# A second pair of blocks in seven products, and another order of gates, branches and output pairs

## The chip, the cores and the metric

The kernel runs on one core of one Trainium2 chip. The metric is the device time of one execution in microseconds (us), and the kernel before takes 769.0 us (median of three: 768.53, 769.0, 769.34). The core's engines are named as in the profile: PE is TensorE (matmuls and transposes), PEld its loads of weights, DVE is VectorE, ACT is ScalarE, POOL is GpSimd and SP is SyncE. POOL and SP do hardly more here than start transfers from device memory, each from a queue of its own.

## The reference

One layer over x of 256 tokens by 2048 channels, in float32:

```python
h = rms_norm(x, pre_norm_w)
proj = h @ w_in                       # 12304 columns, one combined projection
oa = gated_delta_rule(...)            # branch A, 8 heads of 128, from proj
ob = moba_attention(...) * silu(moba_z)   # branch B, 8 heads of 128, from proj
u_a = oa @ w_branch_a                 # 256 x 1024 by 1024 x 2048
u_b = ob @ w_branch_b                 # 256 x 1024 by 1024 x 2048
merged = sigmoid(gate_a) * u_a + sigmoid(gate_b) * u_b    # gates from proj, 2048 columns each
y = merged @ w_out                    # 256 x 2048 by 2048 x 2048
out = x + rms_norm(y, post_norm_w)
```

All that the change touches lies behind the two mixers, from `u_a` on.

## The kernel before, in words

**Precision.** TensorE multiplies at a reduced precision of float32, so each operand is split into a high part (a cast, on ScalarE) and a low part (the difference, on VectorE), and each product is three matmuls: high by high, high by low, low by high. `split` (line 221) does this for weights, 1024 elements a partition at a time, called a part below. It takes the tiles from a pool with three buffers, and every fourth part from a pool with one, so four parts can be in hand. Weights come in as 1 MB tiles `raw_...` from SP's queue, three buffers, two parts each.

**Blocks.** The 2048 columns of a gate, a branch or the output are four blocks of 512 columns; the 256 tokens are two halves. `proj_n` (line 347) computes one block the plain way: for each k tile of 128 and each token half, three matmuls of 512 columns into one PSUM bank. A gate block (k = 2048) is 96 matmuls, a branch block (k = 1024) 48.

**Seven products.** `seven` (line 815) computes two neighbouring blocks over 1024 rows of k at once. It treats token half by k half by column block as a 2 x 2 by 2 x 2 product and uses seven quarter products of 12 matmuls instead of eight, in four PSUM banks. For that it needs four sums of the left quarters (`s_`, each split into high and low) and sums of the weights' quarters (`tq`). The weights' sums are made by `prepare` (line 775): three fetches of 1 MB on GpSimd's queue, four additions on VectorE (`weight_sums`, line 763), and two transfers on GpSimd's queue that add a further quarter in place, one of them started inside `seven` behind product 6. In order of time `seven` runs products 1, 5, 6, 2, 7, 3, 4 and calls `fill(0)` after 1, `fill(1)` after 6, `fill(2)` after 7, `fill(3)` after 3: other products placed beside it, which give ScalarE and VectorE time, as each of its products has only 12 matmuls to two parts of weights. `product` (line 789) runs one such product, for one or two banks.

**Order.** The kernel's text fixes each engine's order. Small generators (`Queue`, line 47) issue side work: each is advanced by `tick`, twice a part, and says by its `yield` how many parts to wait (`T_WAIT` for the weights' sums). `ORDER` (line 43) lists the blocks of the combined projection and the calls of `branch_pair` (`ua0`, `ua1`). From the first branch on TensorE runs:

1. `ua0`: branch A, blocks 0 and 1, in seven products, beside it gate a block 3 (`gate_beside`, line 873);
2. gate b block 0 (`gb0`);
3. `ua1`: branch A, blocks 2 and 3, in seven, beside it gate b block 1;
4. branch B, blocks 0 and 1, the plain way (`branch`, line 1099); `weighted` (line 1089) multiplies them by the gate and adds the other branch; `merge` (line 1148) transposes the merged blocks, splits them, and makes the sums of their quarters;
5. gate b block 2;
6. output blocks 0 and 1, first half of k, in seven, beside it gate b block 3; the four banks are then copied away to SBUF ("parked", `park`, line 1195), as the second half of k needs branch B's last blocks;
7. output blocks 2 and 3, first half of k, in seven, beside it branch B blocks 2 and 3 (`branch_part`, line 1216);
8. the second half of k for output blocks 2, 0, 1 the plain way, the parked banks copied back ahead (`back`, line 1296), and block 3 with its weights split ahead (`last_parts`, `last`).

`weigh` (line 1243) squares a finished block on ScalarE and multiplies it by the norm's weight on VectorE; `finish` (line 1261) takes the root on ScalarE, scales and adds x on VectorE in five pieces, and sends each piece out, the pieces in turn on SP's and ScalarE's queue.

Of the kernel before, what the change touches and what calls it, by code (L numbers as in the profile page):

```python
# [27 lines left out]
T_WAIT = (5, 7, 7, 4)  # L28
# [15 lines left out]
    "q0 mv0 zg0 q1 kq2 kq3 zg1 v0 v1 v2 ga0 zm0 zm1 mv1 v3 mk0 mk1 mk2 mk3 ga1 ga2 ua0 gb0 ua1"  # L44
).split()

# [29 lines left out]
def hybrid_layer(  # L76
# [157 lines left out]
    hT = big.tile([P, KT, 2 * S], F32R, tag="hT", name="hT")  # L234
# [580 lines left out]
    def seven(quarter, s_, tq, w, c, banks, name, fill=lambda i: None, done=lambda b: None):  # L815
# [3 lines left out]
        fill(0)  # L819
        product([s_[0]], tq[0], [c12], [True], f"{name}p5")  # L820
# [32 lines left out]
    def branch_pair(i):  # L853
        c = 2 * i
        while not oas or not formed:
            sq.tick()
            gq.tick()
# [12 lines left out]
        gate = gate_beside(*(("ga", 3, CGA), ("gb", 1, CGB))[i])  # L870
        seven(quarters(oaT[0]), oas, tqs[-1], wa, c, (c11, c12, c21, c22), f"ua{c}", fill=gate, done=done)
# [15 lines left out]
    def next_sums(w, c):  # L887


        for q in aq + bq:  # L890
            q.drain()
        tq = [big.tile([P, 4, 512], F32, tag=f"z{i}", name=f"tq{len(tqs)}_{i}") for i in range(3)]
        prepare(tq, w, c, (2, 0, 1))

    def solve():
# [112 lines left out]
        tq = tg[:, 0], tz, tg[:, 1]  # L1008
# [100 lines left out]
    for blk in ORDER:  # L1109
# [17 lines left out]
        if n == "ua":  # L1127
            next_sums(*((wa, 2), (wo, 0))[c])
# [3 lines left out]

    mT = [big.tile([P, KT // 2, 2 * S], F32R, tag="u1", name="mT_0")]


    sums = [big.tile([P, 2, 4, P], F32R, tag=tg, name=f"sum_{tg}") for tg in ("tt", "tv", "tw")]
    SH = [tl[:, 0] for tl in sums] + [wk.tile([P, 4, P], F32R, tag="s", name="sum4_hi")]
    SL = [tl[:, 1] for tl in sums] + [wk.tile([P, 4, P], F32R, tag="s", name="sum4_lo")]
# [7 lines left out]
    summed, turned_blocks = [], []  # L1146

    def merge(c):
# [18 lines left out]
        if c == 1:  # L1167
# [9 lines left out]
            summed.append(True)  # L1177

    for c in range(2):
        branch(c)  # L1180
        mq.add(merge(c))
    sigmoid_gate("gb", CGB, 2)


    def ready(cond):
        while not cond():
            for q in (dq, sq, wq, mq):
                q.tick()

    ready(lambda: formed and summed)  # L1190
    first_half = quarters(mT[0])
# [24 lines left out]
    def branch_part(c, h):  # L1216
        if h == 0:

            if c == 3:
                ready(lambda: 2 in turned_blocks)  # L1220
            pbs[c] = [aux_tile(f"a_ub{c}_{t}") for t in range(NT)]
        product([ob(0, h), ob(1, h)], load(wb, h, c, "ub"), pbs[c], [h == 0] * 2, f"ub{c}_{h}")
        if h == 1:
            wq.add(weighted(c, pbs[c]))
            mq.add(merge(c))

    def beside_second(i):
        for c, h in (((2, 1),), ((3, 0),), ((3, 1),), ())[i]:
            branch_part(c, h)
# [142 lines left out]
```

## Time and profile before

| | |
|---|---|
| median of three executions | 769.0 us |
| the profiled execution | 769.19 us |
| its span | 767.5 us, TensorE granted 0.996 of full clock |
| TensorE busy | 758.3 us |
| VectorE, ScalarE busy | 564.9 us, 447.8 us |
| bytes moved | 162.36 MB, mean 212 GB/s |

The span is what the profile's records cover; the time is 1.7 us longer. A view by lines gives groups of instructions with their busy time, count and mean length; a view by windows gives the busy time of each engine in a stretch; the chain follows the instruction that ended last back through what released each step. Matmuls overlap, so their busy times add up to more than the time between their starts.

### The profile page before, as it was taken

The page shows a single profiled execution, that of the slowest core. Times are in us where ns is not written, and L with a number is a line of the kernel's source. Part 1 is how long each engine was busy: PE and PEld are TensorE (multiplying, and loading weights), DVE is VectorE, ACT ScalarE, POOL GpSimd, SP SyncE. Part 2 cuts the span into 40 slices and gives each one's busy share as a digit, 9 for nine tenths or more (in the row PEclk, how much of TensorE's full clock was granted, in tenths as well). Part 3 has the DMA queues.
Part 4 walks back from the last instruction along what each step waited for, and adds up shares of the span by engine and source line. Part 5 has one row for each costly group of instructions (what it writes and reads, how often), then busy time and mean ns, then how long its engine had stood idle before and what let it go on. Part 6 is the DMA issues. An engine that isn't in the chain of part 4 may idle for free.

```text
span 767.5 us, 10492 instructions
## 1 busy us (share of the span) xinstructions
PE 758.3 (99%) x3953; PEld 649.2 (85%) x3953; DVE 564.9 (74%) x920; ACT 447.8 (58%) x679; POOL 47.1 (6%) x73
## 2 busy tenths in 40 slices
PE   9999999999999999999999999999999999999995
PEld 8998988899888888888899888788888888888885
DVE  6877669885977898775457876676676976788664
ACT  6776666657655664554556474654555466665562
POOL 4000001112000000003001000100100000100000
PEclk9999999999999999999999999999999999999998
DMA  9585676458655557668437756886798497879732
GB/s 303 177 257 202 192 212 173 137 164 226 189 195 182 190 181 215 172 193 204 131 108 273 212 166 214 241 280 227 215 313 294 161 299 191 332 219 310 289 114 111
DMA packets 99321, 162.36 MB, mean 212 GB/s; under 512 B 3525, under 2 KB 49222, under 8 KB 98758
## 3 DMA queue, kind: packets, MB, share of 16 engines
q1 hardware_dynamic: 89766, 135.46, 54.3%
q0 software_dynamic: 8896, 25.18, 12.7%
q10 hardware_dynamic: 608, 1.06, 0.4%
q8 instruction: 31, 0.51, 0.3%
q14 instruction: 20, 0.16, 0.1%
HBM read 158.52 MB, written 3.15 MB: 211 GB/s over the span
## 4 chain that ended last, share of the span: by engine, by line
PE 96%; ACT 2%; DVE 1%; issue 0%; DVEq 0%; ACTq 0%
PE a_gb L148 11%; PE a_ga L148 11%; PE a_y L148 10%; PE a_zg L148 6%; PE a_mq L148 6%; PE a_v L148 6%; PE a_k L148 6%; PE a_mk L148 6%; PE a_ub L148 6%; PE a_zm L148 6%; PE a_mv L148 5%; PE a_ua L148 5%; PE a_q L148 4%; PE s L148 1%; PE ms L148 1%; PE po L148 1%
## 5 line engine op out<-in xcount | busy, mean ns | idle before, releaser
L148 PE MATMUL a_ga<-hi_ga,hT 128*128 128x512 f32 x256 | 82.1, 394 | 0.0
L148 PE MATMUL a_gb<-hi_gb,hT 128*128 128x512 f32 x256 | 81.5, 392 | 0.0
L148 PEld LDWEIGHTS a_gb<-hi_gb,hT 128*128 128x128 f32 x256 | 48.0, 188 | 10.5
L148 PEld LDWEIGHTS a_ga<-hi_ga,hT 128*128 128x128 f32 x256 | 48.1, 188 | 10.0
L227 DVE TENSOR_TENSOR lo_gb<-raw_gb,hi_gb 128x1024 fp32r<-128x1024 f32 x32 | 39.0, 1223 | 23.6 <-ACT hi_gb L226 23.2
L227 DVE TENSOR_TENSOR lo_ga<-raw_ga,hi_ga 128x1024 fp32r<-128x1024 f32 x32 | 39.0, 1223 | 19.8 <-ACT hi_ga L226 19.4
L226 ACT CAST hi_ga<-raw_ga 128x1024 fp32r<-128x1024 f32 x32 | 33.8, 1055 | 30.3 <-PE a_ga L148 17.4
L148 PE MATMUL a_ga<-lo_ga,hT 128*128 128x512 f32 x128 | 50.1, 391 | 0.1
L226 ACT CAST hi_gb<-raw_gb 128x1024 fp32r<-128x1024 f32 x32 | 33.5, 1051 | 28.3 <-PE a_gb L148 18.0
L148 PE MATMUL a_gb<-lo_gb,hT 128*128 128x512 f32 x128 | 50.0, 391 | 0.0
L148 PE MATMUL a_zg<-hi_zg,hT 128*128 128x348 f32 (+1 forms) x192 | 47.1, 322 | 0.0
L148 PE MATMUL a_mq<-hT,hi_mq 128*128 128x512 f32 x128 | 47.0, 407 | 0.0
L148 PE MATMUL a_mk<-hT,hi_mk 128*128 128x512 f32 x128 | 46.2, 402 | 0.0
L148 PE MATMUL a_q<-hT,hi_q 128*128 128x512 f32 x128 | 45.9, 398 | 0.0
L148 PE MATMUL a_v<-hT,hi_v 128*128 128x512 f32 x128 | 45.3, 398 | 0.0
L148 PE MATMUL a_ub<-hi_ub,obT 128*128 128x512 f32 x128 | 40.8, 392 | 0.0
L148 PE MATMUL a_k<-hT,hi_k 128*128 128x512 f32 x128 | 40.8, 401 | 0.0
L148 PE MATMUL a_zm<-hi_zm,hT 128*128 128x512 f32 x128 | 40.5, 392 | 0.0
L148 PE MATMUL a_mv<-hi_mv,hT 128*128 128x512 f32 x128 | 40.1, 391 | 0.0
L148 PE MATMUL a_v<-hT,lo_v 128*128 128x256 f32 x128 | 36.0, 282 | 0.0
L148 PE MATMUL a_q<-hT,lo_q 128*128 128x256 f32 x128 | 35.9, 280 | 0.0
L148 PE MATMUL a_mq<-hT,lo_mq 128*128 128x256 f32 x128 | 35.9, 280 | 0.0
(398 smaller groups left out, 2008.6 us busy)
## 6 DMA issues: line engine op xcount, KB each, us to landing
raw_ga<-in_w_in_dram SPq DMA_DIRECT2D x16, 1024.0 KB, 5.2
raw_gb<-in_w_in_dram SPq DMA_DIRECT2D x16, 1024.0 KB, 5.2
raw_y<-in_w_out_dram SPq DMA_DIRECT2D x14, 1024.0 KB, 8.6
raw_q<-in_w_in_dram SPq DMA_DIRECT2D x8, 1024.0 KB, 5.6
raw_mv<-in_w_in_dram SPq DMA_DIRECT2D x8, 1024.0 KB, 5.1
raw_v<-in_w_in_dram SPq DMA_DIRECT2D x8, 1024.0 KB, 5.7
raw_zm<-in_w_in_dram SPq DMA_DIRECT2D x8, 1024.0 KB, 5.1
raw_mq<-in_w_in_dram SPq DMA_DIRECT2D x8, 1024.0 KB, 5.7
```

The lines of the kernel that those rows point to most:

```text
L148: return pin(nc.tensor.matmul(*args, **kwargs))
L226: nc.scalar.copy(hi, raw)
L227: nc.vector.tensor_tensor(lo, raw, hi.bitcast(F32), op=ALU.subtract)
```

## The change

Branch B's blocks 0 and 1 are computed by `seven` too. Its left sums are new: `input_sums` joins the attention output's high and low parts, makes the four sums on VectorE and splits them again. Its weights are prepared in the second half of the gate b tile, which is still empty, and two other tiles. The order on TensorE becomes: `ua0` with gate a block 3; `ua1` with gate b block 0; gate b block 1; branch B blocks 0 and 1 in seven with gate b block 2; branch B block 2; gate b block 3; output blocks 0 and 1, first half of k, in seven, with branch B block 3 beside products 1 and 6 and nothing beside the last ones; output block 0, second half; output blocks 2 and 3, first half, in seven, with the rest of output blocks 0 and 1 beside it; output block 2, second half; block 3. No bank is parked. The wait for sums moves into `seven`, ahead of product 5. A square root of a constant is taken behind the last gate. All pieces of the first token half go out by SP's queue. The tile of the normed input becomes two tiles of half its size, each reused on its own.

```diff
-T_WAIT = (5, 7, 7, 4)
+T_WAIT = (5, 4, 4, 7)
...
 ORDER = (
-    "q0 mv0 zg0 q1 kq2 kq3 zg1 v0 v1 v2 ga0 zm0 zm1 mv1 v3 mk0 mk1 mk2 mk3 ga1 ga2 ua0 gb0 ua1"
+    "q0 mv0 zg0 q1 kq2 kq3 zg1 v0 v1 v2 ga0 zm0 zm1 mv1 v3 mk0 mk1 mk2 mk3 ga1 ga2 ua0 ua1"
...
-    hT = big.tile([P, KT, 2 * S], F32R, tag="hT", name="hT")
+    hT = Halves(*(big.tile([P, KT // 2, 2 * S], F32R, tag=f"hT{i}", name=f"hT_{i}") for i in range(2)))
...
         s5 = tq[0][:, 0]
         product([quarter(0, 0)], load(w, 0, c, name), [c21], [True], f"{name}p1")
         fill(0)
+        while not (formed and s_):
+            for q in (dq, sq, iq, wq, mq):
+                q.tick()
         product([s_[0]], tq[0], [c12], [True], f"{name}p5")
         nc.scalar.copy(c11, c21)
         product([s_[1]], tq[1], [c21], [False], f"{name}p6")
...
     def branch_pair(i):
         c = 2 * i
-        while not oas or not formed:
+        while not oas:
             sq.tick()
...
-        gate = gate_beside(*(("ga", 3, CGA), ("gb", 1, CGB))[i])
-        seven(quarters(oaT[0]), oas, tqs[-1], wa, c, (c11, c12, c21, c22), f"ua{c}", fill=gate, done=done)
+        gate = gate_beside(*(("ga", 3, CGA), ("gb", 0, CGB))[i])
+        def beside(j):
+            if j == 3:
+                if i == 0:
+                    z = [z_tile(k, "ua2") for k in range(3)]
+                    prepare(z, wa, 2, (0, 1, 2))
+                else:
+                    gb23 = gb_tile()[:, 2:4].rearrange("p c t n -> p (c t) n")
+                    prepare((gb23, z_tile(0, "ub"), z_tile(2, "ub")), wb, 0, (0, 2, 1))
+            gate(j)
+        seven(quarters(oaT[0]), oas, tqs[-1], wa, c, (c11, c12, c21, c22), f"ua{c}", fill=beside, done=done)
+        if i == 1:
+            iq.add(input_sums())
...
-    def next_sums(w, c):
-        for q in aq + bq:
-            q.drain()
-        tq = [big.tile([P, 4, 512], F32, tag=f"z{i}", name=f"tq{len(tqs)}_{i}") for i in range(3)]
-        prepare(tq, w, c, (2, 0, 1))
+    def z_tile(i, name):
...
+    iq = Queue()
+    extra.append(iq)
+    ob_sums = []
...
+    def input_sums():
+        hi, lo = sum_tiles("obs")
+        l = big.tile([P, 4, 4, P], F32, tag="z1", name="obs_f")
+        l = [l[:, i] for i in range(4)]
+        quarter = quarters(obs[0])
...
+        def part(i):
+            nc.scalar.copy(hi[i], l[i])
+            nc.vector.tensor_tensor(lo[i], l[i], hi[i].bitcast(F32), op=ALU.subtract)
+        yield 2
+        whole(2, 1, 0)
+        whole(0, 1, 1)
+        yield 1
+        less(0, 2, 0)
+        whole(1, 0, 0)
+        yield 1
+        less(2, 1, 2)
+        whole(3, 0, 1)
+        yield 1
+        less(1, 0, 1)
+        part(0)
+        yield 1
+        nc.vector.tensor_tensor(l[3], l[3], l[1], op=ALU.add)
+        part(1)
+        yield 1
+        part(2)
+        yield 1
+        part(3)
+        ob_sums.extend(zip(hi, lo))
...
-        tq = tg[:, 0], tz, tg[:, 1]
+        tq = tg[:, 0], tg[:, 1], tz
...
-        if n == "ua":
-            next_sums(*((wa, 2), (wo, 0))[c])
...
+    sigmoid_gate("gb", CGB, 1)
+    bb = [acc_tile(f"a_ub0_{n}") for n in ("11", "12", "21", "22")]
+    ready_halves = []
+    def weighted_half(b):
+        i = next(i for i in range(4) if bb[i] is b)
+        c, t = i % 2, i // 2
+        nc.vector.tensor_tensor(gb_tile()[:, c, t, :], gb_tile()[:, c, t, :], b, op=ALU.mult)
+        nc.vector.tensor_tensor(ga(c, t), ga(c, t), gb_tile()[:, c, t, :], op=ALU.add)
+        ready_halves.append(c)
+        if ready_halves.count(c) == 2:
+            merged.append(c)
+    ob = quarters(ob_tile())
+    seven(ob, ob_sums, tqs[-1], wb, 0, bb, "ub", fill=gate_beside("gb", 2, CGB), done=weighted_half)
+    prepare([z_tile(i, "y") for i in range(3)], wo, 0, (1, 2, 0))
...
     for c in range(2):
-        branch(c)
         mq.add(merge(c))
-    sigmoid_gate("gb", CGB, 2)
...
-    gate = gate_beside("gb", 3, CGB)
+    branch(2)
+    sigmoid_gate("gb", CGB, 3)
+    root = wk.tile([P, 1], F32, tag="rstd", name="root")
+    pin(nc.scalar.activation(root, epst, AF.Sqrt))
+    while not merged[1:]:
+        wq.tick()
+    mT.append(big.tile([P, KT // 2, 2 * S], F32R, tag="hT0", name="mT_1"))
+    mq.add(merge(2))
+    first_half, second_half = quarters(mT[0]), quarters(mT[1])
     banks = [acc_tile(f"a_y0_{n}") for n in ("11", "12", "21", "22")]
-    def park(b):
-        nc.scalar.copy(freed(next(i for i in range(4) if banks[i] is b)), b)
+    pb = [aux_tile(f"a_ub3_{t}") for t in range(NT)]
     def beside_first(i):
-        if i == 3:
+        if i < 2:
+            product([ob(0, i), ob(1, i)], load(wb, i, 3, "ub"), pb, [i == 0] * 2, f"ub3_{i}")
+        if i == 1:
+            wq.add(weighted(3, pb))
+            mq.add(merge(3))
+            spare = big.tile([P, 2, 4, 512], F32, tag="hT1", name="tq_y2")
             ga01 = ga_[:, 0:2].rearrange("p c t n -> p (c t) n")
-            tq = [big.tile([P, 4, 512], F32, tag=f"z{j}", name=f"tq_{j}") for j in (0, 2)]
-            prepare((tq[0], ga01, tq[1]), wo, 2, (1, 0, 2))
-        gate(i)
-    seven(first_half, list(zip(SH, SL)), tqs[-1], wo, 0, banks, "y", fill=beside_first, done=park)
-    parked = [freed(i) for i in range(4)]
-    tail = big.tile([P, KT, 2 * S], F32R, tag="hT", name="mT_1")
-    mT.append(tail[:, : KT // 2])
-    ob = quarters(ob_tile())
-    pbs = {}
-    def branch_part(c, h):
-        if h == 0:
-            if c == 3:
-                ready(lambda: 2 in turned_blocks)
-            pbs[c] = [aux_tile(f"a_ub{c}_{t}") for t in range(NT)]
-        product([ob(0, h), ob(1, h)], load(wb, h, c, "ub"), pbs[c], [h == 0] * 2, f"ub{c}_{h}")
-        if h == 1:
-            wq.add(weighted(c, pbs[c]))
-            mq.add(merge(c))
-    def beside_second(i):
-        for c, h in (((2, 1),), ((3, 0),), ((3, 1),), ())[i]:
-            branch_part(c, h)
-    c21, c11, c12, c22 = (acc_tile(f"a_y2_{n}") for n in ("21", "11", "12", "22"))
-    branch_part(2, 0)
-    ready(lambda: formed)
-    seven(first_half, list(zip(SH, SL)), tqs[-1], wo, 2, (c11, c12, c21, c22), "y", fill=beside_second)
+            tq_next.extend((spare[:, 0], ga01, spare[:, 1]))
+            fetch(tq_next, wo, 2, (0, 2, 1))
+    tq_next = []
+    seven(first_half, y_sums, tqs[-1], wo, 0, banks, "y", fill=beside_first)
...
-            (nc.sync if i % 2 == 0 else nc.scalar).dma_start(of[t * P : (t + 1) * P, cs], yw[t][:, cs])
...
+            (nc.sync if t == 0 or i % 2 == 0 else nc.scalar).dma_start(of[t * P : (t + 1) * P, cs], yw[t][:, cs])
+    def rest(c, h, pts):
+        product([second_half(t, h) for t in range(NT)], load(wo, 2 + h, c, "y"), pts, [False, False], f"y{c}_{h}")
...
-    second_half = quarters(mT[1])
-    def rest(c, h, banks):
-        product([second_half(t, h) for t in range(NT)], load(wo, 2 + h, c, "y"), banks, [False, False], f"y{c}_{h}")
-    def back(c, bank):
-        pts = [bank(f"a_y{c}_{t}") for t in range(NT)]
-        for t in range(NT):
-            nc.scalar.copy(pts[t], parked[2 * t + c])
-        return pts
-    ready(lambda: 2 in turned_blocks)
-    rest(2, 0, (c11, c21))
     ready(lambda: 3 in turned_blocks)
-    y0 = back(0, aux_tile)
-    rest(0, 0, y0)
-    last_parts(2)
-    rest(2, 1, (c11, c21))
-    rest(0, 1, y0)
+    formed.clear()
+    sq.add(weight_sums(tq_next, wo, 2, 0))
+    c11, c22 = pb
+    c21, c12 = (aux_tile(f"a_y2_{n}") for n in ("21", "12"))
+    def beside_second(i):
+        if i == 0:
+            rest(0, 1, (banks[0], banks[2]))
+        elif i < 3:
+            rest(1, i - 1, (banks[1], banks[3]))
+        else:
+            last_parts(2)
+        if i == 1:
+            for t in range(NT):
+                weigh(0, t, banks[2 * t])
+    rest(0, 0, (banks[0], banks[2]))
+    seven(first_half, y_sums, tq_next, wo, 2, (c11, c12, c21, c22), "y", fill=beside_second)
+    hx = big.tile([P, NT, D], F32, tag="u1", name="hx")
+    for t in range(NT):
+        weigh(1, t, banks[1 + 2 * t])
+    for h in range(2):
+        rest(2, h, (c11, c21))
+        if h == 0:
+            last_parts(3)
+            nc.sync.dma_start(hx, xf.rearrange("(t p) d -> p t d", p=P))
     for t in range(NT):
         weigh(2, t, (c11, c21)[t])
-    y1 = back(1, acc_tile)
-    rest(1, 0, y1)
-    for t in range(NT):
-        weigh(0, t, y0[t])
-    rest(1, 1, y1)
-    last_parts(3)
-    nc.sync.dma_start(hx, xf.rearrange("(t p) d -> p t d", p=P))
-    for t in range(NT):
-        weigh(1, t, y1[t])
```

More of the change, by code (lines that the diff above doesn't have):

```diff
@@ L43, with __init__, __getitem__ @@
 ORDER = (
-    "q0 mv0 zg0 q1 kq2 kq3 zg1 v0 v1 v2 ga0 zm0 zm1 mv1 v3 mk0 mk1 mk2 mk3 ga1 ga2 ua0 gb0 ua1"
+    "q0 mv0 zg0 q1 kq2 kq3 zg1 v0 v1 v2 ga0 zm0 zm1 mv1 v3 mk0 mk1 mk2 mk3 ga1 ga2 ua0 ua1"
 ).split()
+class Halves:
+    def __init__(self, *halves):
+        self.halves = halves
+    def __getitem__(self, i):
+        p, k, *rest = i
+        n = self.halves[0].shape[1]
+        first = k.start if isinstance(k, slice) else k
+        o = first // n * n
+        k = slice(k.start - o, k.stop - o) if isinstance(k, slice) else k - o
+        return self.halves[first // n][(p, k, *rest)]
 class Queue:
@@ L1176, in merge @@
                 nc.vector.tensor_tensor(SL[i], sf[j], SH[i].bitcast(F32), op=ALU.subtract)
-            summed.append(True)
+            y_sums.extend(zip(SH, SL))
     for c in range(2):
-        branch(c)
         mq.add(merge(c))
-    sigmoid_gate("gb", CGB, 2)
[L1185 to L1191, printed above, removed]
-    gate = gate_beside("gb", 3, CGB)
+    branch(2)
@@ L1239, in hybrid_layer @@
     yw = [big.tile([P, D], F32, tag=f"z{1 - t}", name=f"yw_{t}") for t in range(NT)]
-    hx = big.tile([P, NT, D], F32, tag="u1", name="hx")
     ssy = [cst.tile([P, 4], F32, name=f"ssy_{t}") for t in range(NT)]
@@ L1283, in last_parts @@
         raw = load(wo, kb, 3, "y")
+        tl = big.tile([P, 2, 2, 2, 512], F32R, tag=("g0", "hT1")[kb - 2], name=f"keep_{kb}")
         for u in range(2):
-            hi, lo = keep[len(parts)]
+            hi, lo = tl[:, u, 0], tl[:, u, 1]
             pin(nc.scalar.copy(hi, raw[:, 2 * u : 2 * u + 2, :]))
```

24 lines of the change are left out of this document (16 added, 8 removed).

## The prediction

> **What bounds the kernel now.** First the page: busy time, and the chain that ended last. Then that chain in order of time, and stretches of the span, to see whether TensorE ever waits where the change works.
>
> ```profile
> span 767.5 us, 10492 instructions
> PE 758.3 (99%) x3953; PEld 649.2 (85%) x3953; DVE 564.9 (74%) x920; ACT 447.8 (58%) x679; POOL 47.1 (6%) x73
> PE 96%; ACT 2%; DVE 1%; issue 0%; DVEq 0%; ACTq 0%
> ```
>
> ```profile
> core 0: us, PE busy (x) PEld busy (x) DVE busy (x) ACT busy (x) POOL busy (x), PEclk, DMA share, GB/s
> 480.00:506.00 26.00, 25.92 (x115) 20.94 (x114) 17.69 (x18) 17.00 (x21) 2.06 (x2) 1.00 0.84 260
> 506.00:585.00 79.00, 79.00 (x347) 64.74 (x346) 54.25 (x51) 43.83 (x46) 5.62 (x6) 1.00 0.83 265
> 585.00:631.00 46.00, 46.00 (x210) 37.80 (x210) 37.53 (x43) 22.80 (x28) 2.10 (x2) 1.00 0.73 226
> 631.00:687.00 56.00, 56.00 (x246) 45.77 (x245) 40.93 (x38) 35.35 (x40) 4.13 (x4) 1.00 0.84 267
> 687.00:715.00 28.00, 28.00 (x131) 23.01 (x130) 24.17 (x26) 18.21 (x21) 1.86 (x2) 1.00 0.72 226
> 715.00:755.00 40.00, 40.00 (x184) 33.10 (x183) 21.65 (x27) 20.64 (x34) 0.00 (x0) 1.00 0.50 184
> ```
>
> From 480 us to 755 us TensorE is busy all but 0.08 us, at full clock. So a matmul taken out is worth its whole slot, and a new wait costs its whole length. VectorE is next: 24.17 of 28 us in the busiest stretch.
>
> **The matmuls.** The chain prices a slot, and shows one quarter product (12 matmuls), one whole gate block (96) and the transposes of one half block:
>
> ```profile
> 522.32 21.96 PE a_gb L148 x96
> 544.28 2.76 PE a_ua L148 x12
> 585.46 20.56 PE a_ub L148 x90
> 606.02 0.44 PE mt L151 x4
> ```
>
> 20.56 / 90 = 0.229 us a matmul of 512 columns. Blocks 0 and 1 of the second branch are 96 matmuls now; seven quarter products of 12 are 84. The order listing of both programs has 3820 and 3808 TensorE matmuls and transposes: the 12 are the whole difference, since the other pairs were in seven products already. **12 x 0.229 = 2.75 us go.** A matmul lasts 0.39 us in the page's groups, but they overlap; the slot counts.
>
> **The new VectorE work.** The input sums are 12 instructions of 512 elements a partition on VectorE, with four casts on ScalarE; four weights' sums and the product's two corrections come on top. The weights split for each product are VectorE's main load. What an instruction costs in a row of them:
>
> ```profile
> 607.72 1.27 DVE L1092 TENSOR_TENSOR gb<-gb,a_ub 128x512 f32<-128x512 f32 x2
> 712.09 3.49 DVE L227 TENSOR_TENSOR lo_y<-raw_y,hi_y 128x1024 fp32r<-128x1024 f32 x3
> 627.02 1.22 DVE L227 TENSOR_TENSOR lo_yp<-raw_y,hi_yp 128x1024 fp32r<-128x1024 f32 x1
> 628.16 0.68 DVE L1176 TENSOR_TENSOR sum_lo<-gb,sum_hi 128x512 fp32r<-128x512 f32 x1
> 608.32 1.05 ACT L226 CAST hi_gb<-raw_gb 128x1024 fp32r<-128x1024 f32 x1
> 609.26 0.59 ACT L1161 CAST mT<-mt 128x512 fp32r<-128x512 f32 x1
> ```
>
> Two of 512 take 1.27 us, three of 1024 take 3.49 us: in a row they overlap by about 0.08 us, so a 512 costs 0.605 us and a 1024 1.14 us, the last of a row its full 0.68 or 1.22. A cast costs ScalarE 0.94 us (608.32 to 609.26). A part of weights (two k tiles) can be cast only once TensorE is through with the part four before it. With these I laid VectorE's new order against TensorE's, place by place:
>
> 1. *Second pair of the first branch* now follows the first pair with no gate block between. When TensorE ends the first pair's last product, VectorE has the last weighting (0.605), a weights' sum (1.14) and the gate's first low part (1.22): 2.97 us, some 0.2 us after that end, since the result must first be seen. TensorE wants it after 2.75 + 0.23 = 2.98 us. **Wait 0.2 us.**
> 2. *Gate block 1* (22 us): eight low parts, four weights' sums, the weighting and the 12 input-sum instructions: 12 x 1.14 + 13 x 0.605 = 21.5 us in 22.0 us, and VectorE enters up to four parts (5 us) ahead. No wait. The sums end some 12 us before product 5 needs them.
> 3. *Gate block 3.* Let S be the start of branch block 2 on TensorE. Its four transposes (0.44 each) stand inside. The cast of gate part 3 waits for branch part 3: S + 3 x 2.75 + 3 x 0.44 = S + 9.6, with a copy ahead S + 9.9; its low part ends the VectorE queue's claim at S + 12.1. Then stand 12 instructions of 512 (merge, sums of merged quarters, weighting of block 2), one weights' sum, and the low part of gate part 4: 12 x 0.605 + 1.14 + 1.22 = 9.62, so S + 21.7. TensorE wants it at S + 11.0 + 1.76 + 3 x 2.75 + 0.23 = S + 21.2. **Wait 0.5 us**; the next part has 0.605 + 1.14 + 1.22 = 2.97 us against 2.75: **0.2 us** more.
> 4. *End of the first output pair.* Nothing is placed beside its products 3 and 4 any more, so small products, whose 1.14 us low part serves 1.375 us of TensorE, follow each other. Let U be the end of the last branch block's third part. VectorE is free for the run at U + 2.25; 7 x 0.605 + 12 x 1.14 + 1.22 = 19.1 bring it to the second pair's first low parts at U + 21.4. TensorE wants those at U + 2 x 2.75 + 3 x 2.75 + 2 x 0.44 + 5.5 + 1.375 + 0.23 = U + 21.7. No wait, 0.3 us to spare.
>
> Together **+0.9 us**. That such lateness costs TensorE its length is seen once in the trace of before:
>
> ```profile
> 483.24 0.39 PE L148 MATMUL a_ga<-hi_ga,hT 128*128 128x512 f32 x1
> 483.71 0.50 PE L148 MATMUL a_ga<-lo_ga,hT 128*128 128x512 f32 x1
> ```
>
> 0.47 us from start to start instead of 0.23. It stands ahead of the change's first difference, and stays. Bounds of the 0.9: 0 if VectorE is earlier than I laid it; with no overlap at all (0.08 on each instruction) places 1, 3 and 4 give 0.4 + 1.5 + 0.4 + 1.2 = 3.5 us. The overlap is measured, so I stay at 0.9.
>
> **Parking** (four copies out, four back, ScalarE, 0.6 us each) goes: no wait of TensorE stands there in the rows above, so 0 us (bounds 0 and, for one copy back ahead of a product, 0.6 gained). The split of the input's tile into halves, the wait counts and the loop that now holds product 5 back in the writing of the program issue nothing: they set the order and free the half tiles, 0 us.
>
> **The root ahead, and the output queue.** The table load moves from the end to behind the last gate:
>
> ```profile
> 754.68 1.28 ACT L1263 ACT_TABLE_LOAD   x1
> 755.98 0.29 ACT L1263 ACTIVATE rs<-ssy,rb_True 128x1 f32<-128x1 f32 x1
> 756.50 2.87 DVE L1268 SCALAR_TENSOR_TENSOR yw<-yw,rs,hx 128x256 f32<-128x256 f32 x5
> 757.68 1.66 ACTq L1272 DMA_DIRECT2D out_dram<-yw  x2
> 756.59 1.60 PE L148 MATMUL a_y22b<-mT 128*128 128x256 f32 x12
> 758.03 1.60 PE L148 MATMUL a_y22b<-keep,mT 128*128 128x256 f32 x12
> 759.39 0.38 ACT L1248 ACTIVATE jy<-a_y 128x256 bf16<-128x256 f32 x1 [3.12 <-DVE yw L1268]
> 760.48 0.29 ACT L1263 ACTIVATE rs<-ssy,rb_False 128x1 f32<-128x1 f32 x1 [0.25 <-DVE rb_False L1258]
> ```
>
> The 1.28 us is no 1.28 us of gain: the first half of the rows finishes beside TensorE's last products, which end at 758.03 + 1.60 = 759.63, and the second half follows those. What does reach the end: ScalarE, held by two output transfers of the first half, squares a quarter, that was ready when the next began at 756.59, only at 759.39, and the last root waits 0.25 us for what hangs on it. All first-half transfers are SP's now, so ScalarE squares early: **-0.3 us** (bounds 0 and 0.4). At its new place the load delays the cast of the last branch block's second part; two sigmoids (0.6 each), load, root (0.3), two casts (0.5 each), this part's cast and low part are 1.2 + 1.28 + 0.3 + 1.0 + 1.05 + 1.22 = 6.05 us. TensorE wants it 2.75 + 0.88 + 2.75 + 0.23 = 6.6 us after the gate's end, and the first sigmoid starts three matmuls before that end: about 1 us to spare, 0 us.
>
> [...]
>
> **Transfers.** GpSimd's queue gets a fifth set of weights to sum (three fetches and two adding transfers each, 1 MB apiece); SP has one load of weights fewer.
>
> ```profile
> raw_y<-in_w_out_dram SPq DMA_DIRECT2D x14, 1024.0 KB, 8.6
> tq<-in_w_out_dram POOLq DMA_DIRECT2D x8, 1024.0 KB, 8.2
> ga<-in_w_out_dram POOLq DMA_DIRECT2D x2, 1024.0 KB, 9.9
> 560.00:580.00 20.00, 20.00 (x89) 1.00 1.03 359
> ```
>
> On GpSimd's queue the fetch into the second half of the gate tile waits for the first pair's last low part and holds the adding transfer of the second pair behind it, which is wanted some 20 us later: 8.2 us are hidden. Tightest is product 4 of the first output pair: its adding transfer starts after product 6's last low part, and 12.8 us later its cast is due; 8.2 to 9.9 us fit. 0 us.
>
> **Sum:** -2.75 + 0.9 - 0.3 = -2.15. The profiled execution took 769.19 us beside its 767.5 us span, so 767.0; it stands 0.19 over the median of 769.0. Against the median: **766.9 us**.
>
> **The rivals.**
> - *No new wait* (VectorE keeps its lead): 769.0 - 2.75 - 0.3 = 765.9. For it: before has none in 275 us but 0.24. Against: place 3. Chance 0.10.
> - *VectorE eats the gain.* Its instructions take 0.05 us more each in places 3 and 4 (dependent ones wait for each other, say): 16 x 0.05 and 19 x 0.05 - 0.3, about 1.5 us more: 768.4. Without overlap 769.5. For it: place 4 is 19 us of unbroken VectorE work. Chance 0.20.
> [...]
> - *Slower: the output weights come late.* From product 2 of the first output pair to the load of the block beside the second pair's product 1, TensorE runs 26 us, and five loads, three adding transfers and the norm weights' broadcast must land: 9 x 1.05 = 9.44 MB, 363 GB/s. At the 359 GB/s moved in 560 to 580 us this just fits; the load I find tightest has 12 us against the 8.6 us of the row, 3.4 to spare. At 270 GB/s it takes 35 us: 9 - 3.4 = 5.6 us of waiting, 772.5. It ends over 770.5 once 3.6 + 3.4 = 7 us are lost, from 9.44 MB / 33 us = 286 GB/s down. For it: the stage's mean of 267 GB/s; against: that is what was asked for there, not a limit. Chance 0.09.
> - *The change doesn't take the 12 out of the path*: excluded by the order listing and the full TensorE.
>
> **The numbers.** Forecast 766.9, its own range 766.3 to 767.5, chance 0.58. 0.2% is 1.5 us, about what a measurement here can tell from no change, so faster means under 767.5: 0.10 + 0.03 + 0.50 of the forecast = 0.63; slower (over 770.5) 0.09; the rest, 0.28, is the same. From the no-wait case to most of the case in which VectorE eats the gain: 765.8 to 769.3.
>
> **What would show it.** Right: 84 matmuls of the second branch's first pair; TensorE full but for three gaps, 0.2 us at the second pair's first gate part, 0.5 and 0.2 us in gate block 3; no table load in the last 15 us; the end 7.5 us behind the last matmul instead of 7.8. Wrong: ScalarE idle ended by transfers of output weights that TensorE then waits for, or gaps in the first output pair's last products.

## The result, and the profile after

The changed kernel takes **766.8 us** (median of 9 runs, 766.49 to 767.21), the kernel before 768.84 us (9 runs beside it, 768.36 to 769.34). The ratio is 0.9973, with a 95% interval of 0.9964 to 0.9982: 2.0 us, or 0.27%, are gone. Forecast were 766.9 us.

The busy times on the page of the changed kernel, whose span is 765.1 us:

```profile
PE 755.9 (99%) x3941; PEld 646.3 (84%) x3941; DVE 583.2 (76%) x944; ACT 452.7 (59%) x684; POOL 52.0 (7%) x78
```

TensorE has 12 instructions fewer (3953 before), VectorE 24 more and 18.3 us more work. The same view of the span in stretches as for the kernel before:

```profile
core 0: us, PE busy (x) PEld busy (x) DVE busy (x) ACT busy (x) POOL busy (x), PEclk, DMA share, GB/s
506.00:585.00 79.00, 78.88 (x345) 64.31 (x344) 67.26 (x69) 44.87 (x49) 6.99 (x7) 1.00 0.88 277
631.00:687.00 56.00, 55.64 (x254) 45.23 (x253) 45.40 (x51) 34.07 (x42) 5.46 (x6) 1.00 0.83 264
687.00:715.00 28.00, 28.00 (x128) 23.04 (x127) 24.78 (x25) 19.03 (x24) 2.60 (x2) 1.00 0.83 239
655.00:681.00 26.00, 26.00 (x119) 21.41 (x119) 18.14 (x18) 16.87 (x21) 2.84 (x3) 1.00 0.98 302
```

Two stretches have idle time of TensorE, 0.12 and 0.36 us (585 to 631 us has none). The timeline of TensorE shows where (each row: start, length, engine, line, what is written from what; in brackets how long the engine was idle and for whom):

```profile
483.31 0.50 PE L163 MATMUL a_ga<-lo_ga,hT 128*128 128x512 f32 x1
524.48 0.39 PE L163 MATMUL a_gb<-hi_gb,hT 128*128 128x512 f32 x1
524.98 0.50 PE L163 MATMUL a_gb<-lo_gb,hT 128*128 128x512 f32 x1
647.40 0.61 PE L163 MATMUL a_gb<-hi_gb,hT 128*128 128x512 f32 x2
648.38 0.50 PE L163 MATMUL a_gb<-lo_gb,hT 128*128 128x512 f32 x1 [0.36 <-DVE lo_gb L242]
648.72 0.63 PE L163 MATMUL a_gb<-hi_gb,hT 128*128 128x512 f32 x2
754.61 3.04 PE L163 MATMUL a_y22b<-keep,mT 128*128 128x256 f32 x24
```

At 524 us a matmul starts 0.50 us behind the one before instead of 0.23: a gap of 0.27 us. At 647 us two slots last 0.98 instead of 0.46: 0.52 us. The first is at the first low part of the gate block beside the second pair, the forecast's place 1; the second is at the fourth part's low part in gate block 3, its place 3. The slot behind each gap is longer too: 524.98 to 525.32 and 648.38 to 648.72, 0.34 us instead of 0.23.

The best measure of a change here is the time from the last matmul that both kernels wait for in the same place (the first low part at 483 us, ahead of the change) to the end of the last matmul. I call it the work. Before it was 483.71 to 759.63, 275.92 us; now it is 483.31 to 754.61 + 3.04 = 757.65, 274.34 us: **1.58 us less**. Behind it, 1.07 us instead of 1.38 pass from the end of the last matmul to the beginning of the last five output operations: 0.31 less. This is the tail below; the expectations count it up to the end of the span, 7.45 and 7.8 us. The five operations now, then in the kernel before:

```profile
758.72 2.87 DVE L1336 SCALAR_TENSOR_TENSOR yw<-yw,rs,hx 128x256 f32<-128x256 f32 x5
```

```profile
761.01 2.87 DVE L1268 SCALAR_TENSOR_TENSOR yw<-yw,rs,hx 128x256 f32<-128x256 f32 x5
```

Together 1.9 of the 2.0 us. The profiled pair also differ by 0.40 us *ahead* of 483 us, where the change only gives tiles other places.

### The profile page after: what moved, and what is told of

Its sections match the earlier page's. It is cut to its first block, busy times and chain, and to the rows that moved or that the text cites. A ratio compares the mean times of both kernels' runs of the same rounds, so it can differ in the third digit from the quotient of the medians.

```text
span 765.1 us, 10514 instructions
## 1 busy us (share of the span) xinstructions
PE 755.9 (99%) x3941; PEld 646.3 (84%) x3941; DVE 583.2 (76%) x944; ACT 452.7 (59%) x684; POOL 52.0 (7%) x78
## 4 chain that ended last, share of the span: by engine, by line
PE 94%; DVE 3%; ACT 2%; issue 0%; DVEq 0%
PE a_ga L163 11%; PE a_gb L163 10%; PE a_y L163 9%; PE a_ub L163 6%; PE a_zg L163 6%; PE a_mq L163 6%; PE a_v L163 6%; PE a_mk L163 6%; PE a_k L163 6%; PE a_zm L163 6%; PE a_mv L163 6%; PE a_q L163 4%; PE a_ua L163 4%; PE s L163 1%; PE ms L163 1%; PE po L163 1%
## 5 line engine op out<-in xcount | busy, mean ns | idle before, releaser
L163 PE MATMUL a_mk<-hT,lo_mk 128*128 128x256 f32 x128 | 35.8, 280 | 0.0
```

Source lines behind the costliest of these rows:

```text
L163: return pin(nc.tensor.matmul(*args, **kwargs))
```

## The experiments

All are edits of the changed kernel. "Work" is as above; the changed kernel has 274.34 us of it.

**1. The seven products undone in the second branch.**

```
-    seven(ob, ob_sums, tqs[-1], wb, 0, bb, "ub", fill=gate_beside("gb", 2, CGB), done=weighted_half)
+    branch(0)
+    sigmoid_gate("gb", CGB, 2)
+    branch(1)
...            (and no prepare(..., wb, ...), no input_sums(); T_WAIT (5, 4, 7, 7), for one set of sums fewer)
```

> The changed kernel with one part undone: blocks 0 and 1 of the second branch are computed as two plain blocks of 48 matmuls again, in their new place in the order; their weights' sums, the input sums and the adding transfer are gone. TensorE has 12 matmuls more than the changed kernel. Theory (the 12 matmuls are taken out of a path that TensorE sets): 12 x 0.229 = 2.75 us more, less the part of the 0.52 us wait in gate block 3 that goes because VectorE has fewer instructions ahead of it, so 2.3 to 2.75 us over the changed kernel's 766.8, 769.1 to 769.6, with the end of the work still 7.45 us behind the last matmul. Rival (VectorE's work for the seven products eats most of the gain, in waits too short to stand in a row of their own): at most 1.3 us more, 768.1 or less.

Measured: 769.96 us, ratio to the kernel before 1.0013 (1.0004 to 1.0022), 3.2 us over the changed kernel. The work is 483.08 to 757.56 + 3.04 = 760.60, 277.52 us, 3.18 more. That is a little over the theory's span, and far from the rival. TensorE's timeline shows why it is over 2.75 us: the plain form has waits too, at the fourth low part of gate block 3 and, new, at a low part of the last branch block.

```profile
483.08 0.50 PE L163 MATMUL a_ga<-lo_ga,hT 128*128 128x512 f32 x1
650.49 0.50 PE L163 MATMUL a_gb<-lo_gb,hT 128*128 128x512 f32 x1 [0.18 <-DVE lo_gb L242]
671.40 0.50 PE L163 MATMUL a_ub<-lo_ub,obT 128*128 128x512 f32 x1 [0.25 <-DVE lo_ub L242]
757.56 3.04 PE L163 MATMUL a_y22b<-keep,mT 128*128 128x256 f32 x24
```

Counted with the longer slots behind them, and with place 1's gap, which stays, its waits come to 1.5 us, those of the changed kernel to 1.1. So 2.8 us of the 3.18 are the 12 matmuls, against 2.75 by their slots. The run also says that the rest of the change, without the 12, makes the kernel 1 us slower than the one before (769.96 against 768.91 us beside it).

**2 and 3. The weights' sums in gate block 3, earlier and later.**

```
-T_WAIT = (5, 4, 4, 7)
+T_WAIT = (5, 4, 4, 5)        # 2: two half products earlier
+T_WAIT = (5, 4, 4, 8)        # 3: one half product later
```

> The changed kernel with one number changed: the sums of the first output pair's weights, four VectorE instructions of 1024 elements a partition, begin two half products earlier (wait count 5 instead of 7), while the merged quarters are still being summed in gate block 3. The instructions and their number stay. Theory (the 0.52 us gap is TensorE waiting for the fourth low part, because VectorE has a full queue ahead of it, and every 1024 ahead of it costs its 1.14 us): two such instructions now stand ahead of the low part instead of being one and then spread, so the gap grows by 2 x 1.14 = 2.28 to 2.8 us, and the time to 766.8 + 2.2 = 769.0. Rival (TensorE's short gaps are made up for later, or the weights' sums are not what stands ahead of the low part): gap and time as in the changed kernel, 766.8.

> The changed kernel with the same number moved the other way: the sums of the first output pair's weights begin one half product later (wait count 8 instead of 7). Theory: the weights' sum of 1.14 us no longer stands ahead of the late low part, and both gaps in gate block 3 go (0.52 and about 0.1 us in the changed kernel's trace), the 0.27 us gap at the second branch pair's first gate part stays: 766.8 - 0.6 = 766.2. The sums now end one half product later and the adding transfer of the output weights starts that much later; with 8 us from issue to landing and the first output pair's products more than 10 us behind, nothing else waits. Rival (the low part is late for another reason, the four merged sums' casts for one): the gap stays, 766.8. Rival that ends slower: the adding transfer lands late and product 7 of the first output pair waits, a gap of up to 1.4 us behind 668 us.

Measured: earlier 770.58 us (769.23 to 771.82, ratio 1.0019, 1.0010 to 1.0028), later 767.13 us (ratio 0.9975, 0.9965 to 0.9985).

With the sums earlier the gap is as long as forecast. TensorE's timeline, and the granted clock in the 2 us behind the wait (the column after POOL's):

```profile
482.90 0.50 PE L163 MATMUL a_ga<-lo_ga,hT 128*128 128x512 f32 x1
646.95 0.61 PE L163 MATMUL a_gb<-hi_gb,hT 128*128 128x512 f32 x2
650.19 0.79 PE L163 MATMUL a_gb<-lo_gb,hT 128*128 128x512 f32 x1 [2.62 <-DVE lo_gb L242]
650.78 1.05 PE L163 MATMUL a_gb<-hi_gb,hT 128*128 128x512 f32 x2
651.64 0.63 PE L163 MATMUL a_gb<-lo_gb,hT 128*128 128x512 f32 x1
757.57 3.04 PE L163 MATMUL a_y22b<-keep,mT 128*128 128x256 f32 x24
```

```profile
650.00:652.00 2.00, 1.81 (x4) 1.49 (x5) 2.00 (x4) 0.00 (x0) 0.00 (x0) 0.50 1.14 210
```

From 646.95 to 650.19 stand two slots and 2.78 us of waiting, 2.26 more than in the changed kernel: two sums of 1.14 us, to within 0.02. But the work, 482.90 to 760.61, grew by 3.37 us (the median by 3.8). The rest is the clock: behind this wait TensorE is granted 0.50, and the next slots last 0.43 us (650.78 to 651.64 are two). In this execution a wait of 2.8 us costs 1.1 us more than its length. It is no fixed price: the ten executions take 769.23 us at a granted clock of 0.997 over the whole span up to 771.82 us at 0.993. Here a wait of 2.8 us, 2.62 us of it shown as idle, was enough for the half clock. The waits of about 1 us in the runs below left the clock at 1.00 (1.02 us in run 3, granted 1.00 in 669 to 672 us; 1.06 us in run 7, granted 1.00 in 695 to 698 us); what a wait between 1.06 and 2.8 us does, these runs do not show.

With the sums later both gaps in gate block 3 are gone, as the theory said, and yet the time is not shorter: a new gap of 1.02 us stands at the second low part of the last branch block. TensorE, then ScalarE ahead of it:

```profile
668.94 0.50 PE L163 MATMUL a_ub<-lo_ub,obT 128*128 128x512 f32 x1 [0.77 <-DVE lo_ub L242]
662.00 1.05 ACT L241 CAST hi_ub<-raw_ub 128x1024 fp32r<-128x1024 f32 x1 [4.91 <-DMA raw_ub<-in_w_branch_b_dram]
662.95 1.26 ACT L759 ACTIVATE gb<-a_gb,rstd 128x512 f32<-128x512 f32 x2
664.22 1.28 ACT L1280 ACT_TABLE_LOAD   x1
665.51 0.20 ACT L1280 ACTIVATE root<-epst 128x1 f32<-128x1 f32 x1
665.62 1.05 ACT L1256 CAST mT<-mt 128x512 fp32r<-128x512 f32 x2
666.56 1.07 ACT L241 CAST hi_ub<-raw_ub 128x1024 fp32r<-128x1024 f32 x1
```

ScalarE has been idle 4.91 us when the block's first weights land. Then comes an unbroken row: the cast, the two sigmoids, **the table load of the root ahead**, the root, two casts, and only then the second cast for that block. This is the row that the forecast priced for the root's new place, with one thing missing: that a transfer sets its beginning.

In the changed kernel the same row starts with the same kind of wait, and TensorE just gets through:

```profile
661.44 1.05 ACT L241 CAST hi_ub<-raw_ub 128x1024 fp32r<-128x1024 f32 x1 [3.51 <-DMA raw_ub<-in_w_branch_b_dram]
662.40 1.25 ACT L759 ACTIVATE gb<-a_gb,rstd 128x512 f32<-128x512 f32 x2
667.11 1.23 DVE L242 TENSOR_TENSOR lo_ub<-raw_ub,hi_ub 128x1024 fp32r<-128x1024 f32 x1 [0.15 <-ACT hi_ub L241]
668.76 0.39 PE L163 MATMUL a_ub<-lo_ub,obT 128*128 128x512 f32 x1
```

The low part ends at 667.11 + 1.23 = 668.34 and is used at 668.76: 0.4 us to spare. The 0.52 us wait ahead of it had been covering this one. Not all of run 3's 1.02 us was uncovered, though: in its profile the row also starts 0.56 us later (662.00 against 661.44), and why the weights landed later there was not tried. Run 4, below, has the same wait count in this place; its row starts at 661.27 us, and a gap comes all the same.

**4 and 5. All three new gaps, and then the table load.** In 4 the sums of the first branch's second pair are also taken out of the way of place 1; in 5 the root ahead goes as well.

```
-T_WAIT = (5, 4, 4, 7)
+T_WAIT = (5, 2, 4, 8)        # 4 and 5
...
-    root = wk.tile([P, 1], F32, tag="rstd", name="root")
-    pin(nc.scalar.activation(root, epst, AF.Sqrt))        # 5 only
```

> The changed kernel with two wait counts changed: the output weights' sums one half product later as in the run before (8 instead of 7), and the sums of the first branch's second pair two half products earlier (2 instead of 4), so that none of them stands between the last weighting of the first pair and the first low part of the gate block beside the second pair. Theory: all three gaps that the change brought go (0.27, 0.52 and about 0.1 us), 766.8 - 0.9 = 765.9, which is the forecast's rival without any new wait. Rival: VectorE is as full in the neighbouring products, so the waits only move to other low parts, and the time stays at 766.8.

> The run with both wait counts moved (5, 2, 4, 8), with one part of the change undone beside it: no root of a constant is taken ahead, so the table load stands before the first half's root at the end again. In that run a new gap of 0.78 us had come at the last branch block: its second low part follows a ScalarE chain that begins with the first cast of that block's weights, which a late transfer sets (661.27 us), and has the 1.28 us table load and the 0.2 us root in it. Theory (the load in this chain is what makes the low part late): ScalarE is 1.28 + 0.11 = 1.4 us earlier with the second cast, the gap of 0.78 us goes, and since the first half's root has 3 us before the last matmul, the load costs nothing at the end: tail 7.45 us as before, time 766.65 - 0.8 = 765.9. Rival (the weights' transfer itself is too late, and the first low part of the block waits for it): a gap stays at the block's first or second low part, 766.4 to 766.7. Rival on the end (the load holds back the second half's squares): tail about 7.8 us, 766.3.

Measured: 4 takes 766.65 us (ratio 0.9971, 0.9960 to 0.9983), 5 takes **765.82 us** (765.74 to 766.07, ratio 0.9961, 0.9948 to 0.9973). In 4 the gaps at 524 and 647 us are gone and one of 0.78 us from start to start stands behind the table load. So its theory was wrong; the rival had the time, and that the wait moves, but not the cause, which is ScalarE's row and not a full VectorE. In 5 no new gap is left. The gap in 4, then the rows of 5: TensorE, the two casts of the block's weights, and the last five operations (the table load now stands at 751.72 us):

```profile
668.21 0.50 PE L163 MATMUL a_ub<-lo_ub,obT 128*128 128x512 f32 x1 [0.62 <-DVE lo_ub L242]
```

```profile
483.46 0.50 PE L163 MATMUL a_ga<-lo_ga,hT 128*128 128x512 f32 x1
753.63 3.04 PE L163 MATMUL a_y22b<-keep,mT 128*128 128x256 f32 x24
661.69 1.05 ACT L241 CAST hi_ub<-raw_ub 128x1024 fp32r<-128x1024 f32 x1 [4.73 <-DMA raw_ub<-in_w_branch_b_dram]
663.79 1.04 ACT L241 CAST hi_ub<-raw_ub 128x1024 fp32r<-128x1024 f32 x1
757.74 2.87 DVE L1334 SCALAR_TENSOR_TENSOR yw<-yw,rs,hx 128x256 f32<-128x256 f32 x5
```

The weights still end a long idle time of ScalarE, 4.73 us, but the second cast now starts 2.1 us behind the first instead of 4.6 (in run 3's rows). The work is 483.46 to 756.67, 273.21 us. This gives the price of two terms at once. Against the kernel before (275.92) it is 2.71 us less: the 12 matmuls, 2.75 by their slots. Against the changed kernel it is 1.13 us less: what its waits cost. And the tail is 757.74 - 756.67 = 1.07 us, as in the changed kernel: with the load back at the end nothing is lost. Run 5 beats both kernels, by 1.0 us the changed one: its five times all lie below the nine of the changed kernel, which were not taken beside them, and the work says the same.

**6 and 11. The end.** In 6 the first half's output pieces go out on both queues again, with the root still ahead; 11 is run 5 with that same edit, so that both parts that touch the end are undone.

```
-            (nc.sync if t == 0 or i % 2 == 0 else nc.scalar).dma_start(of[...], yw[t][:, cs])
+            (nc.sync if i % 2 == 0 else nc.scalar).dma_start(of[...], yw[t][:, cs])
```

> The changed kernel with one part undone: the first half's output pieces go out on SP's and ScalarE's queues in turn again, as before the change; the root stays ahead. Theory (ScalarE, held by the two transfers of the first half, squares a quarter late, and the last root waits for it): the tail behind the last matmul grows from 7.45 to 7.8 us, 766.8 + 0.35 = 767.15. Rival (what shortened the tail is that the table load no longer delays the first half, so that VectorE and ScalarE are through with it before the last matmul ends): tail 7.45 us, 766.8, since the first half's pieces are now ready 2.5 us earlier than in the kernel before.

> The fastest run so far (5, 2, 4, 8, root at the end, 765.8 us) with the first half's output pieces on both queues again: now both parts of the change that touch the end are undone. Each alone left the tail at 7.45 us. Theory (either part suffices: with the load at the end, the first half is finished 1.28 us later, and only then are ScalarE's two transfers still to be issued when the second half's quarter is ready for its square): tail 7.8 us, as in the kernel before, 766.2. Rival (the 0.37 us of the tail come from neither part): tail 7.45 us, 765.8.

Measured: 6 takes 766.79 us (ratio 0.9975, 0.9964 to 0.9986), nothing lost, as its rival had it; 11 takes 766.17 us (ratio 0.9962, 0.9949 to 0.9976), 0.35 us more than 5, as its theory had it. The square of the second half's first quarter and the last five operations, in 6 and then in 11:

```profile
754.64 3.04 PE L163 MATMUL a_y22b<-keep,mT 128*128 128x256 f32 x24
756.44 0.38 ACT L1316 ACTIVATE jy<-a_ub 128x256 bf16<-128x256 f32 x1 [3.39 <-DVE yw L1336]
758.75 2.87 DVE L1336 SCALAR_TENSOR_TENSOR yw<-yw,rs,hx 128x256 f32<-128x256 f32 x5
```

```profile
753.73 3.04 PE L163 MATMUL a_y22b<-keep,mT 128*128 128x256 f32 x24
756.53 0.38 ACT L1314 ACTIVATE jy<-a_ub 128x256 bf16<-128x256 f32 x1 [3.12 <-DVE yw L1334]
758.15 2.87 DVE L1334 SCALAR_TENSOR_TENSOR yw<-yw,rs,hx 128x256 f32<-128x256 f32 x5
```

In 6 ScalarE is held by the two transfers (it issues them from 754.73 to 756.39) and squares late, at 756.44, but still 1.2 us ahead of TensorE's end at 757.68, and the tail is 1.07 us. In 11 the load has moved the first half 1.28 us back, the square starts 0.24 us before TensorE's end at 756.77, and the tail is 1.38 us, that of the kernel before. The two parts are one and the same 0.31 us: either brings it, both bring no more.

**7. Four more VectorE instructions where it has no pause.**

```
+    for k in range(4):
+        jk = wk.tile([P, 512], BF16, tag="jy", name=f"more_{k}")
+        pin(nc.vector.tensor_tensor(jk, *(mT[0][:, i].bitcast(F32) for i in range(2)), op=ALU.add))
     formed.clear()
```

> The changed kernel with four VectorE instructions of 512 elements a partition added, whose result nobody reads, behind the last block's merge at the end of the first output pair (place 4 of the prediction, where VectorE has no pause from 680.75 to 705 us and the prediction found 0.3 us to spare). Theory: 4 x 0.605 = 2.4 us less 0.3 us to spare, TensorE waits 2.1 us for the low parts of the first output pair's end and the second pair's first product, 768.9. Rival (VectorE's place 4 has more room than worked out, since TensorE shows no gap there at all): 0 to 1 us, 766.8 to 767.8. Rival for the forecast's own case of a slower VectorE (every instruction there 0.05 us longer): the same 2.1 us per 2.4 us added.

Measured: 769.07 us (ratio 1.0003, 0.9994 to 1.0012), 2.3 us more; forecast 768.9. The added row, and the first and the last of TensorE's three waits behind it:

```profile
691.84 2.49 DVE L1362 TENSOR_TENSOR more<-mT 128x512 bf16<-128x512 f32 x4
695.52 0.50 PE L163 MATMUL a_y<-lo_y,mT 128*128 128x512 f32 x1 [0.90 <-DVE lo_y L242]
703.47 0.50 PE L163 MATMUL a_y<-lo_yp,mT 128*128 128x512 f32 x1 [0.15 <-DVE lo_yp L242]
```

The first gap appears 3.7 us behind the beginning of the added work. VectorE's row is 2.39 us later from there on, and the work grows by 2.28 us, 0.11 of it in the slot behind the last wait. So the end of the first output pair has about 0.2 us of VectorE to spare, where the forecast had 0.3.

**8, 9 and 10. More transfers at the beginning of the first output pair.** In 8 two copies of output weights to a scratch tensor:

```
+        if i == 0:
+            for j in range(2):
+                nc.sync.dma_start(more[j], wo[j * 512 : (j + 1) * 512, 0:512])        # 8
+            for j in range(n):
+                nc.sync.dma_start(more[j], tqs[-1][0])        # 9: n = 1; 10: n = 3
```

> The changed kernel with two transfers of 1 MB added on SP's queue, of output weights to a scratch tensor in DRAM that nobody reads, issued ahead of the last branch block's two loads at the beginning of the first output pair. In the changed kernel's profile the stretch from 655 to 681 us has the DMA engines busy 0.98 of the time at 302 GB/s, and ScalarE waits 3.5 us for the first of these two loads. Theory, after the runs so far (these loads are the next bound; 0.4 us to spare at the second low part): 2.1 MB at 302 to 390 GB/s are 5.4 to 7 us, so TensorE waits 5 to 6.6 us, 772 to 773.5, and by the clock's behaviour behind a long wait up to 1.5 us more. The prediction's own figure (3.4 us to spare): 2 to 3.6 us, 768.8 to 770.4. Rival (transfers hidden: what shares the engines only moves waits of ScalarE that TensorE doesn't see): 766.8.

> The changed kernel with one transfer of 1 MB added on SP's queue, between the load of the first output weights and the two loads of the last branch block: a copy of the summed output weights to a scratch tensor in DRAM that nobody reads. Its source is written only at about 650 us, so it can't be taken ahead, as the two transfers of the run before were. Theory (these loads are the next bound, 0.4 us to spare at the block's second low part): 1.05 MB at the 391 GB/s that 660 to 670 us show take 2.7 us, so TensorE waits 2.3 us behind 665 us, 769.1. The prediction's own 3.4 us to spare: hidden, 766.8.

> The same with three such transfers. Theory: 8.1 us at 391 GB/s, TensorE waits 7.7 us, 774.5, and up to 1.5 us more where the wait is long enough for the clock to fall, as it did behind the 2.8 us wait of the second run. The prediction's own 3.4 us to spare: 4.7 us of waiting, 771.5. Transfers hidden: 766.8. Between this run and the one with a single transfer lies the price of a megabyte in this stage: 2.7 us if the engines are the limit.

Measured: 8 takes 766.91 us (ratio 0.9975, 0.9965 to 0.9984), no change, and tells nothing: its copies depend on nothing, so nothing ties them to their written place, and the trace has them at 23.32 us, at the kernel's beginning. With a source that is written only at 650 us they stand where they were meant to: 9 takes 770.0 us (ratio 1.0014, 1.0005 to 1.0023), 10 takes 776.63 us (ratio 1.0100, 1.0086 to 1.0113), both a little over their theories of 769.1 and of 774.5 to 776 us. The cast that starts ScalarE's row, in 9 and then, with the wait it causes and the stretch that holds it, in 10:

```profile
484.16 0.50 PE L163 MATMUL a_ga<-lo_ga,hT 128*128 128x512 f32 x1
665.36 1.05 ACT L241 CAST hi_ub<-raw_ub 128x1024 fp32r<-128x1024 f32 x1 [6.60 <-DMA raw_ub<-in_w_branch_b_dram]
```

```profile
670.96 1.99 ACT L241 CAST hi_ub<-raw_ub 128x1024 fp32r<-128x1024 f32 x2 [4.01 <-DMA raw_ub<-in_w_branch_b_dram]
672.06 0.80 PE L163 MATMUL a_ub<-hi_ub,obT 128*128 128x512 f32 x1 [6.18 <-ACT hi_ub L241]
```

```profile
670.00:681.00 11.00, 8.48 (x23) 6.42 (x24) 4.72 (x4) 4.47 (x5) 0.00 (x0) 0.60 1.03 385
```

Run 9 is 0.85 us late already at 483 us (484.16 against 483.31). Counted from there, the cast starts 3.1 us later with one megabyte and 9.6 us later with three, and the work grows by 2.8 us (484.16 to 761.34) and 10.1 us (483.26 to 767.66). So a megabyte moves the landing by 3.1 to 3.2 us. In 10 clock is lost as well (0.60 in 670 to 681 us); between the two runs' medians lie 3.3 us a megabyte.

Two other causes can be ruled out. SP is not held up by the late source: it issues the block's first load in the same place in all three (653.50 us in the changed kernel, 654.33 in 9, where all is 0.85 later, 653.40 in 10). And it is not only the order in SP's queue. The adding transfer that GpSimd's own queue issues at 650 to 651 us takes longer from issue to landing too. From a view of the transfers issued then (the last number is the us to landing), the changed kernel, 9 and 10:

```profile
tq_y<-in_w_out_dram POOLq DMA_DIRECT2D x1, 1024.0 KB, 8.9
```

```profile
tq_y<-in_w_out_dram POOLq DMA_DIRECT2D x1, 1024.0 KB, 12.8
```

```profile
tq_y<-in_w_out_dram POOLq DMA_DIRECT2D x1, 1024.0 KB, 18.0
```

So the transfers of both queues share what is full here (DMA engines busy 0.98 at 302 GB/s in the changed kernel), and this stage's transfers are at their limit: the last branch block has 0.4 us to spare. The prediction's 3.4 us belonged to a later stretch, from product 2 of this pair to the load beside the second pair's product 1, which these runs do not test by itself.

## Why the prediction was right, step by step

- **The matmuls, -2.75 us.** Right: 2.71 us in run 5, where nothing else stands in TensorE's way.
- **VectorE's waits, +0.9 us.** The right places, a little too small: 1.13 us, forecast 0.9 (the changed kernel against run 5). Place 1 was 0.27 us by its gap, forecast 0.2; place 3 was 0.52, forecast 0.5; the next part lost some 0.1 us in place of 0.2. These gaps add to 0.9. The remaining 0.2 us are the slots behind the two long gaps, 0.34 us instead of 0.23 each: the prediction lets a wait cost its whole length, and it costs TensorE 0.11 us more. Places 2 and 4 have no wait, as forecast. Place 3 follows the count of instructions ahead of the low part, as run 2 shows by two sums' length.
- **The cover behind place 3** was the miss among the sums. The forecast asked what each wait costs, but not what stands right behind it: remove place 3 and another wait takes its place (0.78 us in run 4; 1.02 in run 3, with weights that landed later). The changed kernel's time is not affected by it; an attempt to improve it is.
- **Parking, 0 us.** Not tried by itself. That the kernel without it and without waits (run 5) differs from the one before by the 12 matmuls alone fits 0.
- **The end, -0.3 us.** The size is right (1.38 to 1.07 us), the reason was half of it. The step put it on the transfers' queue alone; runs 6 and 11 show that the earlier load brings the same, and that either suffices.
- **The root's new place, 0 us, about 1 us to spare.** 0 is right for the changed kernel, but only 0.4 us were to spare. The step that failed: the first sigmoid starts three matmuls before the gate's end. The gate ends at 662.14 us, so that would be at about 661.45; it starts at 662.40, behind a cast that waited for a transfer. Nothing in the sum allowed for this cast, so that the rest of the margin held it was luck. The load itself held ScalarE for its 1.28 us and no longer: in run 3's rows the sigmoids end at 664.21 and the load starts at 664.22, the load ends at 665.50 and the root starts at 665.51. The 0.03 in the forecast's sum of chances stood for a load that holds ScalarE longer than that, and no run shows one.
- **Transfers, 0 us.** Right for the time, wrong in the step, and so in part luck. It named the adding transfer for product 4 of the first output pair as the tightest, and its rival counted 3.4 us to spare at a load up to the second pair's product 1; the tightest found here, ahead of both, are the two loads of the last branch block, for the first of which ScalarE waits 3.5 us. The rival of late weights was nearer than its chance of 0.09 says: one megabyte more, and the kernel loses more than it gained.
- **VectorE eats the gain** (rival): its instructions in a row keep their 0.60 us (in run 7 four take 2.49 us, the last of them in full). The rival did not come.

## What to carry to other kernels

Price a wait together with the next one behind it on the same engine: a short wait can cover a second, and removing the first then only uncovers it (with the 0.52 us in gate block 3 gone, run 4 waits 0.78 us behind it). Here each wait of TensorE at full clock also cost about 0.11 us beyond its length (the slot behind it lasts 0.33 to 0.34 us instead of 0.23, in the changed kernel and in runs 1, 3, 7 and 9). A transfer that ends an idle time of ScalarE, even one that TensorE doesn't feel, is the place to measure, by adding one megabyte there, before anything is put into the row behind it. And a table load belongs where the engine is idle *and* the row behind it is not late; at the end of this kernel it cost nothing once the first half's transfers had left ScalarE's queue (run 5), and 0.31 us while two of them were still there (run 11).

## What was not expected of the hardware

In run 2 a wait of 2.8 us halved TensorE's clock for the next slots (granted 0.50 in 650 to 652 us), while waits up to 1.06 us did not (run 7, granted 1.00 in 695 to 698 us); the ten executions of run 2 spread over 2.6 us, the nine of the changed kernel over 0.7. And the stretch ahead of 483 us, the same in all of these runs but 8, varies by itself: the first low part there came at 482.90 us in run 2 and at 484.16 in run 9, more than half of what the whole change brought. Differences below 1 us are better read between two rows of TensorE than from the total.
